# Seven block products for both MLP weights of a hybrid decoder step, with the combinations left in running PSUM banks, on one core

## The chip, the core and the metric

One core of one Trainium2 chip runs the whole program. The metric is the device time of one execution in microseconds (us). Five engines work side by side and wait for one another by semaphores: TensorE (PE, with its weight loads as PEld), VectorE (DVE), ScalarE (ACT), GpSimd (POOL) and SyncE (SP), which issues the transfers. Each of them takes its own instructions strictly in the order in which the program holds them.

## The reference, cut to what matters

One layer over 512 prompt tokens and 64 sample tokens, 576 in all. Two mixers come first and write one matrix; the change touches what follows it.

```python
D_MODEL = 1024
D_FF = 4 * D_MODEL
...
    h1 = x + jnp.concatenate([oa, ob], axis=-1) @ w_o
    hid = jnp.square(jax.nn.relu(rmsnorm(h1, norm2_g) @ w_up))
    y = h1 + hid @ w_down
    return y, kb, vb, s_new, conv_new
```

## The kernel before, in words

Everything is kept transposed: features on the 128 partitions, the 576 tokens along the row, in two halves of 288 (`HALF`). A float32 product is made of three matmuls on numbers split in a high part and the rest: high by high, high by low, low by high. ScalarE writes the high part, VectorE or GpSimd subtracts it to get the low one. A matmul is 128x128 weights by 288 tokens.

**w_up by seven products.** `up(u)` (L1711) makes 256 rows of the hidden layer, for u = 0 to 15. The weights of a unit are seen as 2x2 blocks A11, A12, A21, A22 and the tokens and features as a 2x2 block matrix too, and Winograd's form of Strassen's rule gives the four results from seven products and some sums. The sums of the weights, S1 to S4, are made by GpSimd in `sums_splitter` (L407), four additions of 256 columns for each loaded chunk; `two_parts` (L432) then splits the chunk (1024 columns) and its sums (768) in high and low. The sums of the activations are made once, in `x_factors` (L1619), out of four quadrants `q[0]` to `q[3]` per pair of features i = 0 to 3; `x_parts` (L1641) splits them into the tiles `xf`. Each of the seven products is accumulated over i in a PSUM bank of its own, and `up_out` (L1737) combines them on VectorE, one addition from PSUM per bank. `up_square` (L1757) applies the token scale S and the relu in one VectorE instruction, squares on ScalarE and splits the result into `hid`.

**w_down plainly.** For each 512 hidden rows c and each 128 output rows and half, 12 matmuls run in one bank, and `add_down` (L1776) adds the bank to the residual `h1` on VectorE.

**Order.** The kernel writes its instructions through a class `Flow`, which keeps a clock for each engine by a table of costs and always issues the task that could start first; so the order on each engine is fixed when the program is built. In the MLP the order of the units is two ups, then d(c-2) and two ups in turn, and two downs at the end. Buffers come from pools with caps by use: `mr` for loaded weight chunks, `ms` for weight sums, `q` for quadrants, `g` for PSUM banks (8).

The stage ahead of the MLP is `proj_o`, the product with w_o. Its outputs go through `after_o` (L1560), which adds to `h1`, scales into the quadrants `xq`, and sums the squares for the norm with GpSimd (`acc`, `sq`). So the sums that `up(0)` needs are made while PE still runs `proj_o`.

Of the kernel before, what the change touches and what calls it, by code (L numbers as in the profile page):

```python
# [11 lines left out]
F32R = mybir.dt.float32r  # L12
# [200 lines left out]
def hymba_step(ctx: ExitStack, tc: tile.TileContext, a):  # L213
# [93 lines left out]
    def pool_tt(out, x, y, op, mark=None):  # L307
        fl.op("POOL", 135 + size(x) / 0.47, lambda: nc.gpsimd.tensor_tensor(out, x, y, op=op), mark)  # L308
# [11 lines left out]
    def dma(dst, src, mark=None, slow=1):  # L320
# [17 lines left out]
                      "mr": 2, "ms": 2, "mh": 2, "mg": 2, "ml": 2, "mm": 2})  # L338
# [32 lines left out]
    order = [("u", 0), ("u", 1)]  # L371
    for c in range(2, 8):
        order += [("d", c - 2), ("u", c)]
    order += [("d", 6), ("d", 7)]
    for kind, c in order:
        for i in range(4):
            chunk[kind, c, i] = len(items)
            if kind == "u":
                m, k = 4 * c + i // 2 * 2, i % 2 * 512
                items.append((a["wu"][m:m + 2, :, k:k + 512].rearrange("m p k -> p m k"), 1024))  # L380
            else:
                items.append((a["wd"][c, i], 1024))
    ups = {chunk["u", c, i] for c in range(8) for i in range(4)}
    raw = {}

    def load_w(i):
        src, cols = items[i]
        r = yield from get("wr" if i < MLP else "mr", MID, "wr")
        d = r[:, :cols]
        if len(src.shape) == 3:  # L390
            d = d.rearrange("p (m k) -> p m k", m=src.shape[1])
        dma(d, src, lambda t: raw.update({i: (r, t)}))
# [14 lines left out]
    def sums_splitter():  # L407


        yield lambda: "S" in done  # L410
        for i in range(MLP, len(items)):
            up = i in ups
            if up:
                s = yield from get("ms", MID, "ws")
            yield lambda: i in raw
            r, t = raw.pop(i)
            fl.at(t)
            if up:
                x = r.rearrange("p (m i k c) -> p m k i c", m=2, i=2, k=2)
                A11, A12, A21, A22 = (x[:, j // 2, j % 2] for j in range(4))  # L420
                x = s[:, :768].rearrange("p (j i c) -> p j i c", j=3, i=2)
                S1, S2, S4 = (x[:, j] for j in range(3))
                pool_tt(S1, A21, A22, OP.add)
                pool_tt(A21, A11, A21, OP.subtract)
                pool_tt(S2, S1, A11, OP.subtract)
                pool_tt(S4, A12, S2, OP.subtract)
                fl.spawn(two_parts(i, r, s))
            else:
                fl.spawn(two_parts(i, r, None))
            yield 0  # L430

    def two_parts(i, r, s):  # L432
        out = []
        if i >= MLP + 1 and ("split", i - 1) not in done:
            yield lambda: ("split", i - 1) in done
        for x, n, uh, ul in ((r, 1024, "mh", "ml"), (s, 768, "mg", "mm")):
            if x is not None:
                h = yield from get(uh, MID, "wh", F32R)
                l = yield from get(ul, MID, "wl", F32R)
                act(h[:, :n], x[:, :n])  # L440
                out.append((x, n, h, l))
        sig(("split", i))
        yield 0
        for x, n, h, l in out:
            tt(l[:, :n], x[:, :n], f(h[:, :n]), OP.subtract)
        rel("mr")
        if s is not None:
            rel("ms")
        mark(ready, i, [(h, l) for x, n, h, l in out])

    def splitter():
        for i, (src, cols) in enumerate(items[:MLP]):
# [11 lines left out]
            rel("wr")  # L464

# [1144 lines left out]
    def quad(name):  # L1610
# [3 lines left out]
        return Quad(t)  # L1614


    xf = {}

    def x_factors(i):  # L1619

# [311 lines left out]
```

## Time and profile before

| what | value |
|---|---|
| median of 3 runs (lowest, highest) | 839.0 us (837.73, 839.65) |
| the profiled execution | 836.92 us, span 835.1 us |
| PE busy | 794.9 us, 95% of the span |
| VectorE busy | 569.1 us, 68% |
| ScalarE busy | 342.0 us, 41% |
| GpSimd busy | 276.2 us, 33% |
| granted TensorE clock, mean | 0.982 |

The table is an average over stages. The profiled execution took 1.8 us more than its span, which is what lies around the program, and 2.1 us less than the median. A matmul's busy time covers its way through the array (about 295 ns), so matmuls overlap and PE's rate is read from how many start in a stretch.

### The profile page before, as it was taken

Reading aid. Unit: us, or ns where it says so; the run is one execution under the profiler, and the core shown is the slowest. Engines: PE = TensorE matmul, PEld = TensorE weight load, DVE = VectorE, ACT = ScalarE, POOL = GpSimd, SP = SyncE. Lnnn points to the kernel's source line nnn. Section 1 sums busy time; section 2 is a strip of 40 time slices with the busy share of each in tenths; the row PEclk is TensorE's granted clock in tenths of the full one; section 3 lists DMA queues with packets and bytes.
Section 4 is the critical chain, followed back from the end, with each engine's and each line's share of the span. In section 5 each row is a group of like instructions: output and inputs, shape, how many; then the busy total and the mean of one; then the engine's idle time right before and its main releaser. Section 6 shows DMA issues by size and latency. Waiting matters only on the chain.

```text
span 835.1 us, 15803 instructions
## 1 busy us (share of the span) xinstructions
PE 794.9 (95%) x6299; PEld 730.8 (88%) x6299; DVE 569.1 (68%) x1144; ACT 342.0 (41%) x660; POOL 276.2 (33%) x294
## 2 busy tenths in 40 slices
PE   9999988999999999999866899999999999999998
PEld 8877877878777887879856899999999999999998
DVE  4467278787777875686757785767768586766743
ACT  6538354654232154443552551434325243333410
POOL 4443222243323000132998622233332323333000
PEclk9999999999999999999987999999999999999999
DMA  7722411116778894223002131412223131313312
GB/s 264 150 82 75 151 52 40 46 60 236 254 291 249 292 317 174 108 82 127 26 1 76 53 125 51 139 58 96 88 77 127 51 127 51 126 52 101 127 51 89
DMA packets 53961, 99.05 MB, mean 119 GB/s; under 512 B 12864, under 2 KB 26304, under 8 KB 53888
## 3 DMA queue, kind: packets, MB, share of 16 engines
q1 hardware_dynamic: 53888, 98.05, 35.8%
q8 instruction: 49, 0.80, 0.4%
q14 instruction: 24, 0.20, 0.1%
HBM read 88.15 MB, written 9.69 MB: 117 GB/s over the span
## 4 chain that ended last, share of the span: by engine, by line
PE 72%; POOL 8%; DVE 7%; issue 5%; DMA 4%; ACT 3%; SPq 2%; POOLq 0%; ACTq 0%; DVEq 0%
PE pg L262 52%; PE pa L262 7%; POOL xq L308 3%; SPq L321 2%; POOL acc L308 2%; PE cha L262 2%; DVE y L285 2%; DMA morekv<-in_ck_dram 1%; DMA wr<-in_wk_dram 1%; PE os L262 1%; POOL ws L308 1%; PE ptp L265 1%; PE sc L262 1%; PE cs L262 1%; PE s L262 1%
## 5 line engine op out<-in xcount | busy, mean ns | idle before, releaser
L262 PE MATMUL pg<-hid,wh 128*128 128x288 f32 x1024 | 203.7, 294 | 0.0
L262 PE MATMUL pg<-xf,wh 128*128 128x288 f32 x896 | 183.9, 300 | 8.0 <-DVE xf L278 7.8
L262 PEld LDWEIGHTS pg<-hid,wh 128*128 128x128 f32 x1024 | 164.1, 188 | 0.0
L262 PEld LDWEIGHTS pg<-xf,wh 128*128 128x128 f32 x896 | 147.3, 192 | 9.0 <-DVE xf L278 8.3
L262 PE MATMUL pg<-hid,wl 128*128 128x288 f32 x512 | 151.0, 295 | 0.0
L270 ACT ACTIVATE wh<-wr 128x1024 fp32r<-128x1024 f32 (+1 forms) x104 | 105.1, 1018 | 105.8 <-PE pg L262 46.7
L262 PE MATMUL pg<-xf,wl 128*128 128x288 f32 x448 | 134.5, 300 | 9.5 <-DVE wl L278 9.5
L278 DVE TENSOR_TENSOR h<-pg,h 128x288 f32<-128x288 f32 x160 | 72.5, 454 | 96.7 <-PE pg L262 96.7
L278 DVE TENSOR_TENSOR wl<-wr,wh 128x1024 fp32r<-128x1024 f32 (+1 forms) x89 | 116.6, 1311 | 27.2 <-ACT wh L270 26.7
L308 POOL TENSOR_TENSOR ws<-wr 128x256 f32<-128x256 f32 x32 | 28.8, 900 | 203.5 <-DMA wr<-in_wu_dram 101.2
L262 PEld LDWEIGHTS pg<-hid,wl 128*128 128x128 f32 x512 | 96.1, 188 | 0.0
L262 PEld LDWEIGHTS pg<-xf,wl 128*128 128x128 f32 x448 | 86.1, 192 | 9.9 <-DVE wl L278 9.9
L262 PE MATMUL pg<-xh,wl 128*128 128x288 f32 x256 | 78.1, 305 | 0.0
L262 PE MATMUL pg<-xl,wh 128*128 128x288 f32 x256 | 78.1, 305 | 0.0
L262 PE MATMUL pg<-xh,wh 128*128 128x288 f32 x256 | 78.1, 305 | 0.0
L308 POOL TENSOR_TENSOR wl<-wr,wh 128x1024 fp32r<-128x1024 f32 x15 | 35.9, 2391 | 82.9 <-ACT wh L270 66.3
L278 DVE TENSOR_TENSOR uq<-pg,uq 128x288 f32<-128x288 f32 x96 | 42.2, 454 | 15.6 <-PE pg L262 13.7
L262 PEld LDWEIGHTS pg<-xh,wh 128*128 128x128 f32 x256 | 48.6, 190 | 3.2 <-issue 3.0
L262 PEld LDWEIGHTS pg<-xh,wl 128*128 128x128 f32 x256 | 48.7, 190 | 2.8 <-issue 2.4
L262 PEld LDWEIGHTS pg<-xl,wh 128*128 128x128 f32 x256 | 48.6, 190 | 2.5 <-issue 1.9
L270 ACT ACTIVATE uq<-uq 128x576 f32<-128x576 f32 x32 | 22.0, 686 | 61.7 <-DVE uq L285 61.6
L270 ACT ACTIVATE wh<-ws 128x768 fp32r<-128x768 f32 x32 | 26.9, 840 | 45.6 <-POOL ws L308 17.5
(297 smaller groups left out, 1545.9 us busy)
## 6 DMA issues: line engine op xcount, KB each, us to landing
wr<-in_wu_dram SPq DMA_DIRECT2D x32, 512.0 KB, 3.9
wr<-in_wd_dram SPq DMA_DIRECT2D x32, 512.0 KB, 3.3
morekv<-in_ck_dram SPq DMA_DIRECT2D x20, 512.0 KB, 5.2
morekv<-in_cv_dram SPq DMA_DIRECT2D x20, 512.0 KB, 5.5
wr<-in_wb_dram SPq DMA_DIRECT2D x16, 512.0 KB, 3.8
wr<-in_wo_dram SPq DMA_DIRECT2D x8, 512.0 KB, 5.6
xr<-in_xT_dram SPq DMA_DIRECT2D x8, 288.0 KB, 5.4
h<-in_xT_dram SPq DMA_DIRECT2D x8, 288.0 KB, 6.7
```

The costliest lines, as they stand in the source:

```text
L262: lambda: nc.tensor.matmul(out, lhsT, rhs, start=start, stop=stop, skip_group_check=True))
L265: fl.op("PE", (97, 230), lambda: nc.tensor.transpose(out, in_, ident[:k, :k]))
L270: fl.op("ACT", cost, lambda: nc.scalar.activation(out, in_, func, bias=bias, scale=scale, accum_out=accum), mark)
L278: dve(lambda: nc.vector.tensor_tensor(out, x, y, op=op), out, x, mark=mark)
L285: dve(lambda: nc.vector.scalar_tensor_tensor(out, x, s, y, op0=op0, op1=op1), out, x, 61 if ap(s) else 0, mark=mark)
L308: fl.op("POOL", 135 + size(x) / 0.47, lambda: nc.gpsimd.tensor_tensor(out, x, y, op=op), mark)
L321: fl.op("SP", 4 * slow * size(dst) * dst.shape[0] / 360.0, lambda: nc.sync.dma_start(dst, src), mark)
```

## The change: what it does

Both weights go by seven products now. `down(c, d)` does for 512 hidden rows and 512 output rows what `up` does: two blocks x, seven products each. The products of a pair are no longer seven banks that VectorE combines: product 1 runs in bank A, is read out, product 6 is accumulated on top of it, is read out, then 7, then 4; bank B takes 2, a second bank B takes 5 and then 3 (`seen` makes PE wait for the read). So three banks serve a pair, the order of the products is 1, 2, 6, 5, 7, 3, 4, and each read-out is one result or one term of it.

The weights are split product by product: `part` turns 512 columns into one tile `mw`, high part in front and low part behind, for each of the seven products; `sums` makes S1 to S4 on GpSimd in four additions of 512 columns. The hidden layer needs sums of its quadrants now (`t_sums`), four per unit; `either_tt` puts each on GpSimd or VectorE, by the scheduler's clocks at that moment, as it does the adding of products 1 and 6 of a `down` to `h1`. The first unit (`CLASSICAL = 1`) goes by all eight products, with the loop over i outside, and needs no sums. The scaling of the quadrants by S, eight GpSimd instructions of 576 columns, becomes sixteen VectorE instructions of 288. w_down's chunks come in two transfers of 256 KB each.

```diff
+    def either_tt(out, x, y, op):
+        n = size(x)
+        if fl.free["POOL"] + 1.4 * (135 + n / 0.47) <= max(fl.free["DVE"], fl.now) + 68 + n / 0.96 + 2000:
+            pool_tt(out, x, y, op, slow=1.4)
+        else:
+            tt(out, x, y, op)
...
-                      "mr": 2, "ms": 2, "mh": 2, "mg": 2, "ml": 2, "mm": 2})
+                      "mr": 2, "ms": 2, "mw": 6})
...
+    PO = (1, 2, 6, 5, 7, 3, 4)
+    OF_W = {1: "A11", 2: "A12", 3: "S4", 4: "A22", 5: "S1", 6: "S2", 7: "S3"}
+    CLASSICAL = 1
...
+    def sums(g, A, S):
+        s = yield from get("ms", MID, "ws")
+        t = yield from get("ms", MID, "ws")
...
+        for k, x, y, op in (("S1", "A21", "A22", OP.add), ("S2", "S1", "A11", OP.subtract),
+                            ("S3", "A11", "A21", OP.subtract), ("S4", "A12", "S2", OP.subtract)):
+            X = {**A, **S}
+            pool_tt(S[k], X[x], X[y], op, slow=1.5)
+            mark(sums_at, (g, k), 0)
+            yield 0
+    def part(key, w, x):
+        if key[1] in (3, 5, 6, 7):
+            fl.at(sums_at[key[0], OF_W[key[1]]][1])
+        act(four(w[:, :512]), x)
+        yield 0
+        tt(four(w[:, 512:]), x, four(f(w[:, :512])), OP.subtract)
+        mark(wready, key, w)
...
+    def t_sums(x, key):
+        q = x.q
+        either_tt(q[4], q[2], q[0], OP.subtract)
+        yield 0
+        either_tt(q[5], q[3], q[4], OP.subtract)
+        yield 0
+        fl.spawn(x_parts(x, key, 4, 2), "tsum")
+        either_tt(q[6], q[3], q[2], OP.subtract)
+        yield 0
+        either_tt(q[7], q[1], q[5], OP.subtract)
...
     def x_factors(i):
...
-            pool_tt(x.two(hf), x.two(hf), both(st2["S"], hf), OP.mult)
...
+    def seen(key):
+        if key not in read:
+            yield lambda: key in read
+        fl.at(read[key][1] + LAG)
...
     def up(u):
...
+            if p in (2, 5):
+                B = yield from get("g", [128, 288], "pg")
+            if p in (6, 7, 3, 4):
+                yield from seen(("u", u, {6: 1, 7: 6, 4: 7, 3: 5}[p]))
+            P = B if p in (2, 5, 3) else A
...
     def up_out(u, p, P):
+        if p in (1, 6, 5):
+            act(q[{1: 4, 6: 5, 5: 6}[p]], P)
...
+        o, i, n = {2: (0, 4, 1), 7: (3, 6, 5), 3: (2, 5, 6)}[p]
+        tt(q[o], P, q[i], OP.add)
...
+        stt(q[o], q[o], 0.0, st2["S"][:, c0:c1], OP.max, OP.mult)
...
+    def down_out(g, x, p, P, s):
+        if p in (1, 6):
+            act(s, P)
+            mark(read, key(p), 0)
+            yield 0
+            r, hf = 0, p // 6
+            o = y(r, hf)
+            either_tt(o, o, s, OP.add)
...
+            r, hf = {2: (0, 0), 5: (1, 1), 7: (1, 1), 3: (0, 1), 4: (1, 0)}[p]
+            tt(y(r, hf), P, y(r, hf), OP.add)
```

How the order changes on the engines, as the built programs hold it. First GpSimd, in the middle of the MLP before: `ws` are weight sums, `wr` a loaded chunk.

```order
L308 TENSOR_TENSOR ws<-wr 128x256
L308 TENSOR_TENSOR wr<-wr 128x2x128
L308 TENSOR_TENSOR ws<-ws,wr 128x256
L308 TENSOR_TENSOR ws<-wr,ws 128x256
L308 TENSOR_TENSOR ws<-wr 128x256
```

The four rows come once per chunk of w_up, 32 times, and nothing else of GpSimd's stands between them. The same engine after, between a `down` and an `up`; `uq` are quadrants of a hidden unit, `h` residual rows, `dq` products read out of PSUM.

```order
L308 TENSOR_TENSOR h_3747<-h_3747,dq 128x288
L308 TENSOR_TENSOR h_3787<-h_3787,dq 128x288
L308 TENSOR_TENSOR ws<-ws,wr 128x512
L308 TENSOR_TENSOR ws<-wr 128x512
L308 TENSOR_TENSOR uq<-uq 128x288
L308 TENSOR_TENSOR ws<-wr,ws 128x512
L308 TENSOR_TENSOR uq<-uq 128x288 x2
L308 TENSOR_TENSOR ws<-wr 128x512
L308 TENSOR_TENSOR uq<-uq 128x288
```

Sums of twice the width now stand between additions for the hidden units and the residual: in the whole MLP 124 of 512 columns and 126 of 288, where there were 128 of 256.

VectorE, in the middle of the MLP before, from the end of a `down` to an `up`; `wl` are low parts of weights, `pg` PSUM banks, S the token scale.

```order
L278 TENSOR_TENSOR wl<-wr,wh 128x1024
L278 TENSOR_TENSOR wl<-ws,wh 128x768
L278 TENSOR_TENSOR uq<-pg,uq 128x288 x3
L278 TENSOR_TENSOR uq<-uq,pg 128x288
L285 SCALAR_TENSOR_TENSOR uq<-uq,S 128x576
L278 TENSOR_TENSOR uq<-pg,uq 128x288 x3
L278 TENSOR_TENSOR hid<-uq,hid 128x2x288
```

The same engine after, in an `up`; `mw` is a product's weights, high and low.

```order
L278 TENSOR_TENSOR mw<-ws,mw 128x512 x3
L278 TENSOR_TENSOR hid<-uq,hid 128x576
L278 TENSOR_TENSOR uq<-pg,uq 128x288
L278 TENSOR_TENSOR hid<-uq,hid 128x288
L285 SCALAR_TENSOR_TENSOR uq<-uq,S 128x288
L278 TENSOR_TENSOR mw<-ws,mw 128x512
L278 TENSOR_TENSOR mw<-wr,mw 128x512 x3
L278 TENSOR_TENSOR uq<-pg,uq 128x288
L285 SCALAR_TENSOR_TENSOR uq<-uq,S 128x288
```

Per unit seven additions from PSUM become three and one scaling from PSUM; the low parts, the scalings and the splits of `hid` are more instructions of a smaller width.

PE, at the beginning of `up(0)` before; `xf_4543` and `xf_4544` are the high parts for i = 0, 1 and i = 2, 3 (the low ones are `xf_4545` and `xf_4546`).

```order
L262 MATMUL pg<-xf_4543,wl 128x288
L262 MATMUL pg<-xf_4544,wh 128x288
L262 MATMUL pg<-xf_4546,wh 128x288
L262 MATMUL pg<-xf_4544,wl 128x288
L262 MATMUL pg<-xf_4544,wh 128x288
```

These rows stand after 42 matmuls on i = 0 and 1, where PE turns to i = 2 and 3. The same place after, from the last row of `proj_o` on; each `xf` now holds one i, high and low.

```order
L262 MATMUL pg<-moa,wl 128x288
L262 MATMUL pg<-xf_4539,mw 128x288 x24
L262 MATMUL pg<-xf_4540,mw 128x288 x24
L262 MATMUL pg<-xf_4541,mw 128x288 x24
L262 MATMUL pg<-xf_4542,mw 128x288 x24
L262 MATMUL pg<-xf_4539,mw 128x288 x3
```

The first unit takes its factors in the order in which they are made, one i after the other, and only the second goes through them product by product.

## Rows read from the trace of the kernel before

**Rows 1.** The page's table of engines: busy us (share of span), instructions.
```profile
PE 794.9 (95%) x6299; PEld 730.8 (88%) x6299; DVE 569.1 (68%) x1144; ACT 342.0 (41%) x660; POOL 276.2 (33%) x294
```

**Rows 2.** The chain that ended last, its end: start us, us, what.
```profile
470.47 361.31 PE pg L262 x2710
...
831.80 0.46 DVE h L278
```

**Rows 3.** Busy us (instructions) by stretch, then PE clock, DMA share, GB/s.
```profile
core 0: us, PE busy (x) PEld busy (x) DVE busy (x) ACT busy (x) POOL busy (x), PEclk, DMA share, GB/s
395.00:447.60 52.60, 34.71 (x220) 33.16 (x220) 35.45 (x37) 27.30 (x53) 50.01 (x44) 0.80 0.07 21
447.60:480.00 32.40, 28.68 (x190) 27.86 (x190) 22.10 (x34) 14.64 (x22) 21.51 (x24) 0.90 0.21 66
480.00:820.00 340.00, 340.00 (x2565) 340.00 (x2565) 232.40 (x357) 121.44 (x151) 92.80 (x98) 1.00 0.28 91
```

**Rows 4.** PE in order of time, 428.7 to 446: start, us, [idle before <-releaser].
```profile
436.28 0.61 PE L262 MATMUL pg<-xf,wl 128*128 128x288 f32 x1 [6.33 <-DVE wl L278]
...
445.04 0.61 PE L262 MATMUL pg<-xf,wh 128*128 128x288 f32 x1 [7.35 <-DVE xf L278]
```

**Rows 5.** VectorE in order of time, pieces from 432 to 549.
```profile
432.51 1.98 DVE L278 TENSOR_TENSOR xf<-xq,xf 128x576 fp32r<-128x576 f32 x1 [3.02 <-ACT xf L270]
434.41 1.81 DVE L278 TENSOR_TENSOR wl<-wr,wh 128x1024 fp32r<-128x1024 f32 x1
...
520.17 1.36 DVE L278 TENSOR_TENSOR wl<-wr,wh 128x1024 fp32r<-128x1024 f32 x1
521.46 1.50 DVE L278 TENSOR_TENSOR wl<-ws,wh 128x768 fp32r<-128x768 f32 x1
...
544.28 0.75 DVE L285 SCALAR_TENSOR_TENSOR uq<-uq,S 128x576 f32<-128x576 f32 x1
544.95 1.77 DVE L278 TENSOR_TENSOR wl<-wr,wh 128x1024 fp32r<-128x1024 f32 x1
546.64 0.44 DVE L278 TENSOR_TENSOR h<-pg,h 128x288 f32<-128x288 f32 x1
547.01 0.92 DVE L278 TENSOR_TENSOR hid<-uq,hid 128x576 fp32r<-128x576 f32 x1
```

**Rows 6.** GpSimd in order of time, the same pieces.
```profile
433.83 1.30 POOL L308 TENSOR_TENSOR acc<-acc,sq 128x288 f32<-128x288 f32 x1
435.10 2.39 POOL L308 TENSOR_TENSOR xq<-xq,S 128x576 f32<-128x576 f32 x1
...
520.53 1.60 POOL L308 TENSOR_TENSOR wr<-wr 128x256 f32<-128x256 f32 x1
...
523.63 0.73 POOL L308 TENSOR_TENSOR ws<-wr,ws 128x256 f32<-128x256 f32 x1
...
544.64 0.99 POOL L308 TENSOR_TENSOR ws<-wr 128x256 f32<-128x256 f32 x1 [15.41 <-DMA wr<-in_wu_dram]
545.72 1.60 POOL L308 TENSOR_TENSOR wr<-wr 128x256 f32<-128x256 f32 x1
```

**Rows 7.** VectorE's groups by shape, 480 to 820: busy us, mean ns.
```profile
L278 DVE TENSOR_TENSOR h<-pg,h 128x288 f32<-128x288 f32 x120 | 54.5, 454 | 73.9 <-PE pg L262 73.9
```

**Rows 8.** GpSimd's groups by shape, 395 to 447.6.
```profile
L308 POOL TENSOR_TENSOR xq<-xq 128x288 f32<-128x288 f32 x16 | 17.8, 1129 | 0.3
L308 POOL TENSOR_TENSOR xq<-xq,S 128x576 f32<-128x576 f32 x8 | 13.6, 1696 | 2.0 <-ACT xq L270 2.0
L308 POOL TENSOR_TENSOR acc<-acc,sq 128x288 f32<-128x288 f32 x11 | 12.5, 1140 | 0.0
```

**Rows 9.** VectorE's groups by shape, 395 to 447.6.
```profile
L278 DVE TENSOR_TENSOR xf<-xq,xf 128x576 fp32r<-128x576 f32 x12 | 15.5, 1308 | 7.6 <-ACT xf L270 7.6
L278 DVE TENSOR_TENSOR wl<-wr,wh 128x1024 fp32r<-128x1024 f32 x4 | 6.6, 1642 | 0.0
L278 DVE TENSOR_TENSOR wl<-ws,wh 128x768 fp32r<-128x768 f32 x3 | 5.3, 1757 | 0.0
```

More of the change, by code (lines that the diff above doesn't have):

```diff
@@ L432, in two_parts @@
[L432 to L442, printed above, removed]
-        yield 0
[L444 to L449, printed above, removed]
+    PO = (1, 2, 6, 5, 7, 3, 4)
@@ L1619, in x_factors, with x_parts, have @@
+    def x_parts(x, key, j, n):
+        s, t = x.t[j // 2][:, j % 2 * 288:(j % 2 + n) * 288], x.out
+        act(high(t, j, n), s)
+        yield 0
+        tt(low(t, j, n), s, f(high(t, j, n)), OP.subtract)
+        for k in range(j, j + n):
+            mark(parts, key + (k,), 0)
+        yield 0
+    def have(key, js):
+        return all(key + (j,) in parts for j in js)
     def x_factors(i):
-        if i >= 2:
-            yield lambda: ("xf", i - 2) in done
         x = hx[i] = yield from quad("xq")
+        x.out = xf[i]
@@ L1654, in hymba_step @@
-    parts = {}
+        yield from t_sums(x, ("x", i))
+        yield lambda: have(("x", i), range(8))
+        rel("q", "q", "q", "q")
     ims1 = ct([128, 5], "ims1")
@@ L1704, in stats2, with three @@
         rel("k", "k")
-        cap.update(g=8)
         sig("R2b")
-    hid, Q = {}, {}
+    hid, Q, read, left = {}, {}, {}, {}
+    LAG = 240
+    def seen(key):
+        if key not in read:
+            yield lambda: key in read
+        fl.at(read[key][1] + LAG)
+    def three(p, w, c, x, j, first, last):
+        c = slice(c * 128, c * 128 + 128)
+        l = w[:, 512:]
+        mm(p, w[:, c], high(x, j), first, False, extra=8)
+        mm(p, w[:, c], low(x, j), False, False, extra=8)
+        mm(p, l[:, c], high(x, j), False, last, extra=8)
@@ L1774, in up_square @@
-        rel("q", "q", "q", "q")
-    def add_down(m, hf, p, last):
-        c0, c1 = HALF[hf]
-        tt(h1[m][:, c0:c1], p, h1[m][:, c0:c1], OP.add)
-        rel("g")
-        if last:
-            yield 0
-            dma(a["yT"][:, m, c0:c1], h1[m][:, c0:c1])
+        sig(("Q", u))
+        for hf in (0, 1):
+            yield lambda: all(("relu", u, hf, r) in done for r in range(2))
+            d = x.t[hf][:, :576]
+            act(d, d, AF.Square)
+        yield 0
+        x.out = hid[u] = yield from get("big", [128, 4608], "hid", F32R)
@@ new lines, in up_square, with down @@
+        fl.spawn(x_parts(x, ("h", u), 0, 2))
+        fl.spawn(x_parts(x, ("h", u), 3, 1))
+        yield from t_sums(x, ("h", u))
+        yield lambda: have(("h", u), OF_X.values())
+        rel("q", "q", "q", "q")
+    def down(c, d):
+        A, B = {}, {}
+        g = ("d", c, d)
+        s = yield from get("q", [128, NT], "dq")
+        for p in PO:
+            w = yield from weights(g, p)
+            for x in range(2):
+                if p in (1,):
+                    A[x] = yield from get("g", [128, 288], "pg")
+                if p in (2, 5):
+                    B[x] = yield from get("g", [128, 288], "pg")
+                if p in (6, 7, 3, 4):
+                    yield from seen(g + (x, {6: 1, 7: 6, 4: 7, 3: 5}[p]))
+                P = B[x] if p in (2, 5, 3) else A[x]
+                for i in range(2):
+                    j = OF_X[p]
+                    yield from factor(("h", 2 * c + i), j)
+                    three(P, w, 2 * x + i, hid[2 * c + i], j, i == 0 and p in (1, 2, 5), i == 1)
+                    yield 0
+                fl.spawn(down_out(g, x, p, P, blk(s, x)), "out")
+            rel("mw")
```

322 lines of the change are left out of this document (180 added, 142 removed).

## The prediction

> **What bounds the kernel now.** I read the page first: PE is busy 95% of the span, GpSimd 33% [rows 1]. Then the end of the chain of waits: from 470.47 us one unbroken run of 2710 matmuls, and after the last of them only one addition and the transfer out [rows 2]. So the MLP is bound by PE. The view by stretches gives its rate: 2565 matmuls in 340 us, 132.6 ns each at clock 1.00, while VectorE is busy 232.4 us, ScalarE 121.4 and GpSimd 92.8 [rows 3]. On those numbers fewer matmuls shorten the kernel and the others have room.
>
> Ahead of it lies a stretch that is not PE's. From 395 to 447.6 PE is busy 34.7 of 52.6 us at clock 0.80, GpSimd 50.0 [rows 3]; PE stands for 6.33 and 7.35 us there, for VectorE's low parts [rows 4]. Its cause decides this case. In [rows 5, 6] the reader should lay VectorE's and GpSimd's instructions side by side. An addition of 256 columns on GpSimd takes 0.73 us by itself (523.63) and 1.60 us at 520.53; it ends at 522.13, which is 0.60 after VectorE's low part of 520.17 ended (521.53). VectorE's next one then ends at 522.96, 0.83 after GpSimd's end. At 544.64 GpSimd ends at 545.63, VectorE's low part 1.09 later (546.72), GpSimd's next 0.60 later (547.32), VectorE's next 0.61 later (547.93). So an instruction of VectorE with both operands in SBUF and one of GpSimd never go on together: each finishes a full hold after the other's end. The addition from PSUM at 546.64 takes 0.44 under a running GpSimd instruction, and 120 of its kind 454 ns on the mean [rows 7]: with an operand in PSUM nothing is waited for.
>
> **Holds.** From [rows 5, 6], as the time from the other's end to the own one. GpSimd: 256 columns 0.60; 288 columns 0.64 (435.13 after 434.49); 576 columns 1.27 (437.49 after 436.22); between the last two, an estimate for 512 columns of 1.13. VectorE: 1024 columns 1.09, 768 0.83, 576 0.61; by their slope of 1.07 ns a column, 512 columns 0.54 and 288 columns 0.30. Shapes of 512 don't stand in the trace of before, so these two are the estimates on which the sum turns; the bounds are below.
>
> **The change part by part.**
>
> PE. w_down loses 1536 - 16x84 = 192 matmuls, the first unit gains 12. 180 fewer at 132.6 ns are 23.9 us, if PE stays the bound. An `up` or a `down` of 84 matmuls needs 11.13 us, the two together (a pair) 22.27.
>
> Shared holds of a pair, counted from the code and the order. `up`, GpSimd: four sums of 512 and four of 288 columns, 4x1.13 + 4x0.64 = 7.08. VectorE: seven low parts of 512, three of 576 and one of 288 for `hid`, three scalings of 288, 7x0.54 + 3x0.61 + 4x0.30 = 6.81. `down`: GpSimd 7.08 again (four sums, four additions of products 1 and 6), VectorE 3.78 for seven low parts. 24.75 us a pair, against 22.27 for PE. Before, two ups and one d (the work of two pairs, 360 matmuls, 47.7 us) held 16x0.60 on GpSimd, and on VectorE eight low parts of 1024 (8x1.09), four of 768 (4x0.83) and eight instructions of 576 (8x0.61): 26.5 us, 56% of PE's time. After it is 111%. The shared holds become the bound; that is the forecast.
>
> VectorE's own time. It starts its next instruction 0.67 us after one of 576 columns (544.28 to 544.95) and 0.37 after one from PSUM (546.64 to 547.01) [rows 5], 0.06 above the hold; so 0.60 for 512 and 0.37 for 288. `up`: 7x0.60 + 3x0.67 + 4x0.37, and four reads of PSUM at 0.37: 9.17. `down`: 4.20 and ten reads of PSUM: 7.90. 17.07 a pair. GpSimd's 14.16 us of holds can hide under VectorE's reads of PSUM alone (14x0.37 = 5.2); the rest, 9.0, VectorE waits. 26.0 us a pair, if it never idles for anything else.
>
> The start. From 395 to 447.6 the holds were, by [rows 8, 9]: GpSimd 16x0.64 + 8x1.27 + 11x0.64 and the other 9 of its 44 instructions, of 256 columns, 5.4: 32.8; VectorE 12x0.61 + 4x1.09 + 3x0.83 and three of 288: 15.1. 47.9 of 52.6 us, 91%. So that is how well two saturated engines share. After, the order has ahead of the last quadrants that `up(0)` needs: GpSimd 12 sums and 9 squares of 288 and two sums of 512, 15.7; VectorE 16 scalings of 288, 13 splits of 576, three low parts of 1024 and six of 512, 19.2. 34.9 at 91% is 38.4, to 433.4. Then the last quarter of `up(0)`, 24 matmuls, at the lower clock level (half rate) 6.4: `up(0)` ends near 440, and some 9 us of holds are still owed (four sums, five squares, three splits, 7.6; the first unit's own 4.7; less 3.4 made ahead for the second). Before, 2796 matmuls remained after it, 370.7 us back from the last one: 461. The start gives 21 us.
>
> The sum. 15 ups and 16 downs are 15.5 pairs. From 440: 15.5x26.0 + 9 = 412, to 852; then as before 3.3 us from the last addition (831.80) to the span's end and 1.8 around the span. 857 against the profiled 836.9, 20 us slower. The bounds of that term: holds packed without a gap, 15.5x24.75 + 9 = 393, to 833 and 838 in all; holds at the 91% of the start, 431, to 876 in all. I take 857, between them, because VectorE's reads of PSUM are spread through every unit [rows 7], as cover for GpSimd needs, and were few in the start.
>
> The Trainium skill, "SBUF — State Buffer", section "SBUF: two separate sides", calls the ports that VectorE (with two SBUF inputs) and GpSimd share an exclusive lock: who starts first has it for the whole instruction, the other fully blocks. The trace agrees in kind, but the blocked one ends 0.60 us after the release, not its whole 0.73. If all of an instruction lay behind the release, each of the 16 GpSimd instructions of a pair would hold 0.13 longer, and the packed sum would be 15.5x26.8 + 9 = 424, 869 in all, in place of 838.
>
> The rest costs nothing while its cover lasts. ScalarE's seven high parts and its reads of 288 columns: it is busy 36% of the MLP now [rows 3], and even doubled it stays under a pair; without that cover its extra work would stand on PE's path. Transfers in halves: share 0.28 of the queues [rows 3], loaded a unit ahead; uncovered, one more landing per chunk. The norm's scaling R2 is needed only by the first reads.
>
> **The rivals.**
>
> (a) PE stays the bound: the two engines overlap more than I count. 440 + 15.5x22.27 = 785, 790 in all. For it: PE is never late from 480 on [rows 3], and GpSimd works only 27% there. Against: every pair of rows above. It decides if a pair's holds come to 22.3 or less, that is if a sum of 512 columns holds under 0.82 us in place of 1.13.
>
> (b) The hand-back of a bank. PE may go on in a bank only after the read. Between a product and its successor in the bank lie 12 matmuls in `up` (1.59 us), 18 in `down` (2.39). ScalarE reads seven of the twelve in a pair and doesn't share holds; VectorE reads five, one in `up` and four in `down`. If two blocked low parts (2x1.67) stand ahead of the read (0.45), PE is late by 2.2 and 1.4 us, 7.8 a pair. What is queued behind PE is every later product. Half of that on top of PE's 22.27 is 26.2, no more than the forecast; all of it 30.1, 15.5x30.1 + 9 = 476, 921 in all; three quarters 28.1, 890. It decides above 3.7 us a pair.
>
> (c) PE's clock. In the gaps its granted clock may fall, as in the start: 0.80 with PE busy 66%, 0.90 with 89% [rows 3]. At 0.80 a pair takes 27.8 us, 885 in all. In the forecast PE is busy 86%; it decides below a mean of 0.86.
>
> (d) The scheduler's order packs the holds as if without a gap: 838, no change or a hair faster.
>
> **How the numbers follow.** The forecast, 841 to 880, 62%; (a) 7%, (b) 12%, (c) 10%, (d) 9%, of which I give 5 to faster and 4 to no change. The median of the runs shown is 2.1 above the profiled execution, so I predict 859. 832 to 892 leaves out (a) and the far part of (b) and (c). A run of this kernel can tell 0.2% from no change: faster 0.12, same 0.04, slower 0.84.
>
> **What would show it.** GpSimd busy over 85% of the MLP (14.2 of holds, and waiting for VectorE in between); its 512-column sums near 1.7 us on the mean, VectorE's 512-column low parts near 1.2 in place of 0.68; both nearer their own time would prove (a). PE busy some 86% from 450 on, its gaps ended by VectorE: by `mw` if the low parts are late, by readers of `pg` if (b) is right. Clock near 1.00; under 0.9 speaks for (c). PE at the second unit by 440 to 447. Wrong it would be if the holds of 512 columns are shorter than read off, or if VectorE idles for ScalarE or PE and the holds fit in those gaps.

## The result, and the profile after

The changed kernel takes 898.0 us (median), the one before 839.25 beside it: a ratio of 1.069, with an interval of 1.065 to 1.073. The prediction was 859, so the direction is right and the loss is three times as large, 59 us in place of 20. Of its four executions one, at 915.8, ran at a lower clock (0.932, the others 0.949 to 0.957) and is left out of the ratio. The profiled execution took 899.43, its span is 897.7.

The page's table of engines, and the shares of the chain that ended last, as [rows 1]:

```profile
PE 806.5 (90%) x6119; PEld 731.5 (81%) x6119; DVE 719.0 (80%) x1317; ACT 418.3 (47%) x910; POOL 476.9 (53%) x407
...
PE 43%; DVE 26%; POOL 11%; issue 9%; ACT 7%; DMA 3%; SPq 0%; DVEq 0%; POOLq 0%; ACTq 0%
```

The chain's last 100 us, where [rows 2] had one run of 2710 matmuls:

```profile
789.04 2.94 POOL ws L308 x2
798.87 3.12 DVE mw L278 x4
817.01 4.64 DVE mw L278 x3
822.08 3.26 PE pg L262 x12
...
858.89 35.44 PE pg L262 x264
```

PE bounds only the last stretch, where only `down`s are left (GpSimd still makes sums until 883.8); before it weight sums and low parts stand in the chain. By stretches, with the columns of [rows 3]; the first matmul of the second unit starts at 441.7, the last one ends at 894.3:

```profile
395.00:441.70 46.70, 40.01 (x268) 39.00 (x268) 43.22 (x56) 27.44 (x55) 36.49 (x28) 0.89 0.07 24
480.00:820.00 340.00, 295.59 (x2016) 286.28 (x2016) 305.84 (x419) 162.22 (x322) 253.59 (x190) 0.93 0.23 75
...
441.70:894.30 452.60, 387.31 (x2621) 375.74 (x2619) 402.59 (x553) 213.71 (x424) 332.50 (x253) 0.92 0.23 75
```

In 340 us PE runs 2016 matmuls where it ran 2565. It is busy 87% of them (86% was predicted), VectorE 90%, GpSimd 75% at a granted clock of 0.93. PE's waits from 441.7 to 894.3 (us, times, longest) add up to 64 us:

```profile
PE pg L262 <- DVE uq L278: 28.7, 10, 4.6
PE pg L262 <- ACT uq L270: 18.8, 11, 4.1
PE pg L262 <- ACT dq L270: 8.7, 3, 7.9
PE pg L262 <- DVE mw L278: 4.2, 3, 2.5
PE pg L262 <- DVE h L278: 3.8, 7, 1.6
```

Most of them are waits for somebody who reads a bank (`uq`, `dq`, `h`), which looks like rival (b). The groups by shape, 480 to 820 (busy us, mean ns, idle before), show something else:

```profile
L278 DVE TENSOR_TENSOR mw<-wr,mw 128x512 fp32r<-128x512 f32 x72 | 90.0, 1279 | 0.6 <-ACT mw L270 0.6
L278 DVE TENSOR_TENSOR mw<-ws,mw 128x512 fp32r<-128x512 f32 x95 | 85.8, 912 | 17.1 <-ACT mw L270 16.9
L308 POOL TENSOR_TENSOR ws<-wr 128x512 f32<-128x512 f32 x48 | 77.2, 1608 | 17.0 <-issue 9.5 <-DVE mw L278 6.7 <-PE pg L262 0.7
L308 POOL TENSOR_TENSOR h<-h,dq 128x288 f32<-128x288 f32 x47 | 54.4, 1176 | 48.3 <-ACT dq L270 45.6 <-ACT mw L270 2.6
L278 DVE TENSOR_TENSOR h<-pg,h 128x288 f32<-128x288 f32 x120 | 51.0, 447 | 8.5 <-POOL h L308 3.7 <-PE pg L262 3.4 <-POOL ws L308 0.3
L308 POOL TENSOR_TENSOR uq<-uq 128x288 f32<-128x288 f32 x47 | 50.6, 1081 | 23.6 <-ACT uq L270 22.5 <-DVE uq L278 0.4
```

What has both operands in SBUF takes longer than by itself (a low part of 512 columns that nothing holds up takes 0.69, at 523.02 in the next piece), and the addition from PSUM stays at 447 ns, as in [rows 7]. VectorE in order of time from the end of an `up` on, then GpSimd:

```profile
523.02 0.69 DVE L278 TENSOR_TENSOR mw<-ws,mw 128x512 fp32r<-128x512 f32 x1 [0.94 <-ACT mw L270]
...
529.05 4.64 DVE L278 TENSOR_TENSOR mw<-wr,mw 128x512 fp32r<-128x512 f32 x3
533.62 0.45 DVE L278 TENSOR_TENSOR uq<-pg,uq 128x288 f32<-128x288 f32 x1
534.10 0.46 DVE L285 SCALAR_TENSOR_TENSOR uq<-uq,S 128x288 f32<-128x288 f32 x1
534.48 0.75 DVE L278 TENSOR_TENSOR hid<-uq,hid 128x576 fp32r<-128x576 f32 x1
...
537.41 0.46 DVE L285 SCALAR_TENSOR_TENSOR uq<-pg,S 128x288 f32<-128x288 f32 x1 [1.32 <-PE pg L262]
```

```profile
529.75 1.72 POOL L308 TENSOR_TENSOR ws<-wr 128x512 f32<-128x512 f32 x1
531.44 1.70 POOL L308 TENSOR_TENSOR ws<-wr,ws 128x512 f32<-128x512 f32 x1
541.14 2.02 POOL L308 TENSOR_TENSOR h<-h,dq 128x288 f32<-128x288 f32 x2 [7.99 <-ACT dq L270]
```

Two lessons stand in these rows. GpSimd's two sums end at 531.47 and 533.14, 1.67 apart, with one low part of VectorE's between them: the predicted holds, 1.13 + 0.54, are 1.67. And the low part ends at 533.69, 0.55 after the sum. But then, from 533.14 to 541.14, GpSimd stands 8 us for a product that ScalarE has yet to read out, and VectorE, which now never waits for it, has little that is ready: its instructions that share fill 4.8 of the 8 us. For the rest the shared resource lies idle. Laying all instructions of the two engines over each other from 441.7 to 894.3, I find 409.7 us in which at least one of them is in an instruction that holds or waits for it, 23.5 in which VectorE reads PSUM while GpSimd is idle, and 19.4 in which both are idle. The first figure is nearly the 412 that the prediction gave to this part, with every read of PSUM covered and no idling; the other 43 are the miss. VectorE itself idles 50.0 us there, mostly for these:

```profile
DVE mw L278 <- ACT mw L270: 18.4, 20, 1.5
DVE h L278 <- PE pg L262: 6.9, 21, 1.0
DVE uq L285 <- PE pg L262: 6.3, 6, 1.3
DVE h L278 <- POOL h L308: 5.2, 6, 1.6
DVE uq L285 <- ACT S L270: 3.3, 1, 3.3
DVE hid L278 <- ACT hid L270: 3.1, 5, 0.7
DVE uq L278 <- PE pg L262: 1.8, 1, 1.8
```

### The profile page after: what moved, and what is told of

The parts are those of the page before. It is cut to its first block, busy times and chain, and to the rows that moved or that the text cites. A ratio compares the mean times of both kernels' runs of the same rounds, so it can differ in the third digit from the quotient of the medians.

```text
span 897.7 us, 16132 instructions
## 1 busy us (share of the span) xinstructions
PE 806.5 (90%) x6119; PEld 731.5 (81%) x6119; DVE 719.0 (80%) x1317; ACT 418.3 (47%) x910; POOL 476.9 (53%) x407
## 4 chain that ended last, share of the span: by engine, by line
PE 43%; DVE 26%; POOL 11%; issue 9%; ACT 7%; DMA 3%; SPq 0%; DVEq 0%; POOLq 0%; ACTq 0%
PE pg L262 23%; DVE mw L278 9%; PE pa L262 7%; POOL ws L308 6%; DVE hid L278 3%; DVE y L285 3%; POOL h L308 3%; DVE uq L285 2%; ACT mw L270 1%; PE cha L262 1%; DVE uq L278 1%; DVE h L278 1%; DMA wr<-in_wk_dram 1%; ACT uq L270 1%; POOL uq L308 1%
## 5 line engine op out<-in xcount | busy, mean ns | idle before, releaser
L262 PE MATMUL pg<-xf,mw 128*128 128x288 f32 x1356 | 214.2, 321 | 58.3 <-DVE uq L278 28.7
L262 PEld LDWEIGHTS pg<-xf,mw 128*128 128x128 f32 x1356 | 204.5, 210 | 66.1 <-DVE uq L278 31.8
L262 PE MATMUL pg<-hid,mw 128*128 128x288 f32 x1344 | 190.2, 302 | 13.3 <-ACT dq L270 8.7
L262 PEld LDWEIGHTS pg<-hid,mw 128*128 128x128 f32 x1344 | 185.6, 194 | 17.5 <-ACT dq L270 9.5
L278 DVE TENSOR_TENSOR mw<-ws,mw 128x512 fp32r<-128x512 f32 x124 | 115.1, 938 | 17.6 <-ACT mw L270 17.4
L270 ACT ACTIVATE mw<-ws 128x512 fp32r<-128x512 f32 x124 | 74.7, 624 | 102.6 <-POOL ws L308 79.4
L278 DVE TENSOR_TENSOR mw<-wr,mw 128x512 fp32r<-128x512 f32 x97 | 118.7, 1251 | 1.0 <-ACT mw L270 1.0
L308 POOL TENSOR_TENSOR ws<-wr 128x512 f32<-128x512 f32 x62 | 98.7, 1593 | 30.3 <-DVE mw L278 10.3
L308 POOL TENSOR_TENSOR h<-h,dq 128x288 f32<-128x288 f32 x63 | 71.9, 1160 | 54.0 <-ACT dq L270 48.7
L308 POOL TENSOR_TENSOR uq<-uq 128x288 f32<-128x288 f32 x63 | 68.0, 1086 | 32.4 <-ACT uq L270 31.3
```

The lines of the kernel that those rows point to most:

```text
L262: lambda: nc.tensor.matmul(out, lhsT, rhs, start=start, stop=stop, skip_group_check=True))
L270: fl.op("ACT", cost, lambda: nc.scalar.activation(out, in_, func, bias=bias, scale=scale, accum_out=accum), mark)
L278: dve(lambda: nc.vector.tensor_tensor(out, x, y, op=op), out, x, mark=mark)
L308: fl.op("POOL", (135 + size(x) / 0.47) * slow, lambda: nc.gpsimd.tensor_tensor(out, x, y, op=op), mark)
```

## The experiments

My theory was the one on record: the shared holds (*ports*). Its rivals were the *hand-back* of a running bank (b) and, once that had fallen, a *chain*: that the sums are late for those who wait for them, and their load matters little. All runs are compared by T, from the second unit's first matmul to the last matmul, since in e5 to e9, e12, e13 and e16 the granted clock was 0.61 to 0.80 between 300 and 350 us, ahead of the MLP, where the run of after has 1.00; with it the second unit starts later, by 20 us in e5 whose order is that of after, which is in the total and not in T. So where a range was given for the total, T is held against it as well. Apart from e4 and e8, each experiment is one execution. A pair is an `up` and a `down`; where holds are given, they are those measured in after, 1.15 and 0.667 us for GpSimd's 512 and 288 columns, 0.549, 0.615 and 0.317 for VectorE's 512, 576 and 288: 25.3 us a pair, where 24.75 was estimated.

| run | us | T | holds a pair | VectorE busy in T | GpSimd busy in T | clock in T |
|---|---|---|---|---|---|---|
| before | 839 | 379.0 | | 255.5 | 109.3 | 1.00 |
| after | 898 | 452.6 | 25.3 | 402.6 | 332.5 | 0.92 |
| e1 no sums | 809.5 | 366.6 | 16.1 | 308.7 | 129.2 | 0.98 |
| e2 bank per product | 892.9 | 444.3 | 25.3 | 403.3 | 333.3 | 0.95 |
| e3 PSUM additions | 915.6 | 464.9 | 22.7 | 408.1 | 259.7 | 0.92 |
| e5 memsets | 840.0 | 373.3 | 16.1 | 314.3 | 252.7 | 0.98 |
| e6 sums unused | 918.2 | 456.9 | 25.3 | 399.9 | 331.5 | 0.93 |
| e7 order knows holds | 925.3 | 464.4 | 25.3 | 387.7 | 321.9 | 0.90 |
| e9 four tiles | 924.5 | 453.7 | 25.3 | 403.1 | 331.3 | 0.95 |
| e10 seven tiles | 1009.8 | 562.9 | 25.3 | 400.3 | 311.6 | 0.90 |
| e11 no PSUM additions | 889.2 | 445.5 | 25.3 | 356.2 | 328.3 | 0.93 |
| e12 all 288 on VectorE | 928.0 | 453.5 | 22.5 | 431.6 | 195.2 | 0.94 |
| e13 quarter fewer sums | 872.3 | 415.8 | 23.0 | 379.3 | 285.0 | 0.98 |
| e14 half the sums | 841.4 | 393.0 | 20.7 | 355.4 | 229.8 | 0.98 |
| e15 sums on their own | 903.0 | 459.8 | 25.3 | 411.3 | 337.2 | 0.93 |
| e16 later additions | 950.4 | 490.3 | 25.3 | 411.8 | 321.4 | 0.89 |

**e1: no weight sums.** Products 3, 5, 6 and 7 are split from plain blocks.

```diff
...
-            pool_tt(S[k], X[x], X[y], op, slow=1.5)
...
```

> The changed kernel without the weight sums: GpSimd's 124 additions of 512 columns are left out, and the products that should use S1 to S4 split a plain block in their place, so the results are not the reference's; every split, product, read-out and hand-back of a bank is still there. Theory of the shared ports (VectorE with two SBUF operands and GpSimd wait for each other): the holds of an up and a down together fall from 25.3 us (with the holds of the trace of after: GpSimd 512 columns 1.15, 288 columns 0.67; VectorE 512 columns 0.55, 576 columns 0.615, 288 columns 0.32) to 16.1, under PE's 22.3, and PE becomes the bound: 435 + 15.5 x 22.3 + 5, that is 785 to 805 us. Theory of the hand-back (PE is late because only 12 or 18 matmuls lie between a product and its successor in a bank, whatever the other engines do): PE's waits for read-outs stay near 60 us, 860 us or more.

809.5 us, a little over the 785 to 805 of the ports. PE is the bound again, busy 355.5 of 366.6 us. So w_up and w_down by seven with running banks, without the sums, would have been faster than before. With every hand-back still there, it isn't the cause.

**e2: a fresh bank for each product.** Each product takes a new bank, so PE never waits for a read-out to go on in one.

```diff
-                yield from seen(("u", u, {6: 1, 7: 6, 4: 7, 3: 5}[p]))
-            P = B if p in (2, 5, 3) else A
+            P = yield from get("g", [128, 288], "pg")
...
```

> The changed kernel with a fresh PSUM bank for each product: nothing is accumulated on top of an earlier product and PE never waits for a read-out in order to go on in a bank; all read-outs and additions stay as they are, so the combinations are left out of the results. Theory of the shared ports: the holds are the same, so the time is nearly the same, 870 to 895 us, and PE's waits turn to the low parts of the weights. Theory of the hand-back: the 60 us of waits for read-outs and the low clock behind them go, 800 to 835 us.

892.9 us. PE's waits move and hardly shrink; the longest from 440 on:

```profile
PE pg L262 <- DVE mw L278: 41.5, 30, 4.0
PE pg L262 <- ACT mw L270: 8.0, 5, 5.7
```

The readers of banks were only the first to be late. With them out of the way the low parts are what PE waits for, and a pair takes 28.1 in place of 28.6 us. Rival (b) falls as the cause.

**e3: products 1 and 6 of a `down` added from PSUM by VectorE.** GpSimd loses four additions a pair.

```diff
-            act(s, P)
...
-            either_tt(o, o, s, OP.add)
+            tt(y(r, hf), P, y(r, hf), OP.add)
```

> The changed kernel with products 1 and 6 of a down added to h1 by VectorE straight from PSUM, in place of a ScalarE read-out and a GpSimd addition; same results. Shared ports: 2.7 us of holds less for each up and down (25.3 to 22.7), VectorE has 1.5 us more of its own; at the 89% packing of the changed kernel 25.5 us, 441 + 15.5 x 25.5 + 9 + 5, about 850 us (835 to 865). Hand-back: VectorE reads nine hand-backs in place of five, and it is the engine with the longer queue: no gain, 895 us or more.

915.6 us, slower, with 2.7 us fewer holds a pair. The expectation of the ports (835 to 865) fails; that of the hand-back, 895 or more, holds. VectorE's own work rose by 1.5 us a pair, it now reads nine of the twelve hand-backs, and PE waits 41.5 us for its `uq` and 25.9 for its `hid`; which of the two makes the loss is not shown. A count of holds by itself is no forecast when the work goes to VectorE instead.

**e4: w_down by all eight products, without its sums.** `up` stays as changed.

```diff
-            if g[0] == "u" and g[1] < CLASSICAL:
+            if g[0] == "d" or g[1] < CLASSICAL:
...
```

> The changed kernel with w_down by all eight block products and no sums for it (16 x 96 matmuls in place of 16 x 84, no weight sums for w_down and no sums of hidden quadrants); w_up as changed; same results. Shared ports: holds of an up and a down 12.8 us against 23.9 of PE: PE is the bound, 441 + 15.5 x 23.9 + 5, 805 to 825 us, 2 to 4% faster than the kernel before. Hand-back: the waits in the ups (47 of some 60 us) stay, about 860 us.

845.8 us against 842.6, ratio 1.003 (1.000 to 1.007). Nearly all of the 59 us come with w_down. That no gain is left was not expected: T is 395.6 us for the 2796 matmuls that took 379.0 before. The first two of these units take 32.3 us (442.1 to 474.4) where they took 30.2 before (452.8 to 483.0), so the start accounts for 2 of the 16.6. All that follows takes 363.3 in place of 348.8, and there PE waits 10.2 us, in 7 waits, for VectorE's `uq`, the hand-back.

**e5: memsets in the place of sums.** Each sum of 512 columns becomes four GpSimd memsets of 256 into the same tile: the same order and waits, the sums are constants.

```diff
-            pool_tt(S[k], X[x], X[y], op, slow=1.5)
+            def sets(t=S[k]):
+                for h in (0, 2, 0, 2):
+                    nc.gpsimd.memset(t[:, h:h + 2], 0.5)
+            fl.op("POOL", (135 + 512 / 0.47) * 1.5, sets)
```

> The changed kernel with each of GpSimd's 124 additions of 512 columns replaced by four memsets of 256 columns into the same tile, which read nothing from SBUF; the order on every engine and every wait stay as in the changed kernel, the weight sums are constants, so the results are not the reference's. Shared ports: the low parts of VectorE no longer wait for the sums; holds of an up and a down fall to 16.1 us and PE (22.3) is the bound, 800 to 825 us, and the low parts of 512 columns return to about 0.68 us. If it is the chain of buffers and engines in itself (GpSimd makes a unit's sums late, ScalarE and VectorE split them late, PE waits) and not the waiting of the two engines for each other: the memsets take a similar time, 870 us or more.

```profile
L475 POOL MEMSET ws<- 128x256 f32 x432 | 113.2, 310 | 26.3 <-DVE mw L278 20.1 <-PE pg L262 6.2
L278 DVE TENSOR_TENSOR mw<-ws,mw 128x512 fp32r<-128x512 f32 x109 | 82.1, 762 | 10.0 <-ACT mw L270 9.9
L278 DVE TENSOR_TENSOR mw<-wr,mw 128x512 fp32r<-128x512 f32 x81 | 66.1, 842 | 1.7 <-ACT mw L270 1.7
```

A sum's place takes 4x0.31 = 1.24 us of GpSimd, about what a sum takes alone; yet T is 373.3, 79 less than after, and VectorE's low parts fall from 1279 and 912 to 842 and 762 ns (480 to 800). GpSimd's time is not the matter, only what it does in it: the memset's row has no source, so it reads nothing from SBUF. The total, 840.0, is above the range expected for the ports because the second unit starts 20 us later, after the clock of 0.61 between 300 and 350. The Trainium skill, "SBUF — State Buffer", section "SBUF: two separate sides", says that a VectorE instruction with two SBUF inputs contends only with a GpSimd operation that reads SBUF; the trace agrees.

**e6: sums made and not used.** The load stays, the products are split from plain blocks.

```diff
-                fl.spawn(part((g, p), w, S[k] if k[0] == "S" else A[k]))
+                fl.spawn(part((g, p), w, A[{"S1": "A22", "S2": "A11", "S3": "A21", "S4": "A12"}.get(k, k)]))
```

> The changed kernel with all weight sums made by GpSimd as before, at the same places of its queue, but the four products that should use them split a plain block in their place, so nothing waits for the sums and the results are not the reference's. The load on the shared ports is the same (25.3 us of holds for an up and a down). Shared ports as a pure throughput: 880 to 900 us as the changed kernel. Chain (the holds alone would pack closer to 25.3, but each unit's sums, splits and products wait for one another, and the blocked instructions lengthen each step): cutting the chain at the sums lets the engines pack, 845 to 870 us, not under the 849 that holds without a gap give.

918.2 us in all, over both ranges, with the second unit at 456.2; T 456.9 against 452.6. Nothing is split from a sum, and the time is the same, which speaks against the chain. But ScalarE's high parts still wait 80.8 us for GpSimd's `ws`: a tile that GpSimd wrote or read comes back as a tile for split weights, and its next user waits for GpSimd all the same. So this run didn't take away what it was meant to; e15 does.

**e7: a scheduler that knows the waiting.** `Flow` delays an instruction that shares until the other engine's ends.

```diff
+        if c.queue[0][2].__name__ == "port":
+            ahead = self.port
...
+        if emit.__name__ == "port":
+            self.port = t - 60
```

> The changed kernel with another order: the scheduler's clocks now let an instruction of VectorE with both operands in SBUF and one of GpSimd wait for each other, in place of factors 1.4 and 1.5 on GpSimd alone; same instructions but for the choice between GpSimd and VectorE, same results. Shared ports as a pure throughput: 885 to 905 us. Chain: an order made with the real delays puts the reads of PSUM in front of blocked low parts and wins some of the 3 us a pair that are not held by anyone, 855 to 885 us.

925.3 us, T 464.4. The order it writes is worse by 12 us, and no expectation held.

**e8: the parts that gain.** w_down plainly as in e4, a bank per product and VectorE's combinations in `up` as before; new against the kernel before are mainly the split by product, and the first unit by all eight.

```diff
...
+            tt(q[5], P, q[4], OP.add)
...
+            tt(q[7], P, q[5], OP.add)
...
```

> w_down by all eight products as in the run with the plain down, and w_up's seven products each in a bank of its own, combined on VectorE as in the kernel before; first unit by all eight, weights split by product; same results. Expected of all theories of the ports: the holds stay under PE's time, and the 1.0 us that each up lost to the hand-back of banks goes: 442 + 15 x 11.13 + 16 x 12.73 + 5 = 818, with some 5 us lost in the second and third unit 820 to 830 us, 1.5 to 2.5% faster than the kernel before. If the loss in the second and third unit (10 us with the plain down) is of the ports of the start: 830.

831.1 us against 840.2: ratio 0.988 (0.986 to 0.990), 1.2% under the kernel before, and well under the changed one. Against e4, T falls from 395.6 to 379.4. 4 of the 16 us are in the first two units (28.1 for 32.3); the other 12 (351.3 for 363.3) are the price of running banks, so (b) was real where the holds don't cover it. T is as before (379.0, for the same 2796 matmuls), so the gain must lie ahead of the second unit. The trace kept doesn't show it: this execution took 838.3 us, with the clock at 0.80 between 300 and 350 and the second unit at 453.7, against 452.8 before. In e4, with the same first unit and the clock at 1.00 there, the second unit begins at 442.1.

**e9 and e10: four and seven tiles for split weights.** A pair might take longer because PE, ScalarE and VectorE hand six tiles round.

```diff
-                      "mr": 2, "ms": 2, "mw": 6})
+                      "mr": 2, "ms": 2, "mw": 4})
...
```

> The changed kernel with four tiles for split weights in place of six; every instruction and every result stays. Theory of the ports: the shared holds (25.3 us a pair) and VectorE's reads of PSUM set 28.6 us a pair, so two tiles fewer change little: 895 to 905 us. Theory of the ring: a pair takes 28.6 in place of 26.0 because PE, ScalarE and VectorE hand six tiles round, and a late low part comes back as a late high part for VectorE; then four tiles must cost clearly: over 920.

> The changed kernel with seven tiles for split weights, at the price of three in place of four for loaded chunks; all results stay. Theory of the ring: VectorE's 51 us of idle time shrink by a third or more, 875 to 888 us. Theory of the ports: 893 to 905.

With four, T is 453.7, 1 us more than after: there is no such ring. The total of 924.5 would fit it (over 920), but the second unit starts at 465.7 here, 24 us later than in after, behind a clock of 0.64 between 300 and 350. Seven tiles cost a loaded chunk: T 562.9, and PE waits 83.7 us for VectorE's and 46.0 for ScalarE's `mw`. A chunk is held until product 4, a unit's last, so with three the next unit's splitting begins late. That says nothing on the ring.

**e11: w_down's additions from PSUM left out.**

```diff
-            tt(y(r, hf), P, y(r, hf), OP.add)
             mark(read, key(p), 0)
```

> The changed kernel without VectorE's ten additions from PSUM in each down (products 2, 5, 7, 3, 4 are run and not added: left out). The shared holds stay all; VectorE loses 10x0.37 = 3.7 us a pair of work that needs no port, and GpSimd as much cover. Theory of the ports: what VectorE saves it waits instead, 890 to 905 us. Theory of VectorE's queue (what it does in order, ports or not, is the limit): 28.6 falls by 2.5 to 3.7 a pair, 840 to 860 us.

889.2 us, T 445.5. VectorE is busy 46 us less and the time falls by 7. Its own queue isn't the limit in after; most of what it saved it stands idle (89 us for 50), and the low parts wait a little longer (1328 and 988 ns).

**e12: all additions of 288 columns on VectorE.**

```diff
-        if fl.free["POOL"] + 1.4 * (135 + n / 0.47) <= max(fl.free["DVE"], fl.now) + 68 + n / 0.96 + 2000:
-            pool_tt(out, x, y, op, slow=1.4)
-        else:
-            tt(out, x, y, op)
+        tt(out, x, y, op)
```

> The changed kernel with all additions of 288 columns on VectorE, so that GpSimd has only the sums of 512; all results stay. Eight a pair move: the holds fall from 25.3 to 25.3 - 8x0.667 + 8x0.317 = 22.5 us a pair, VectorE's own work rises by 8x0.37 = 3.0. Theory of the ports, at the 88% of now: 25.4 a pair, 845 to 855 us. Theory of VectorE's queue: 28.6 rises by 1 to 3 a pair, 910 to 945.

928.0 us, T 453.5: neither the gain of the one nor the loss of the other. The total lies in the range of VectorE's queue only because the second unit starts at 469.3, behind a clock of 0.68 between 300 and 350. VectorE is busy 431.6 of T, 95%. So the likely reading is that the holds gave way and VectorE took their place; that the time came out the same is chance.

**e13 and e14: fewer sums.** Of a unit's four sums S3, then S3 and S4 are left out (the cut is of e14).

```diff
...
-            pool_tt(S[k], X[x], X[y], op, slow=1.5)
+            if k not in ('S3', 'S4'):
+                pool_tt(S[k], X[x], X[y], op, slow=1.5)
```

> The changed kernel with one of the four weight sums per unit (S3) left out, 31 of 124; its product is split from a plain block, so results differ. Theory of the ports with 88.5% packing: 25.3 - 2x1.15 = 23.0 us of holds a pair, 23.0/0.885 = 26.0, 15.5x26.0 + 9 = 412 in place of 452.6 from the second unit to the last matmul, 855 to 870 us in all. Theory that something else holds a pair at 28.6 (the runs so far lie at 445 to 465 whatever was moved): 445 to 460 for that part, 890 to 910 us.

> As the run before, with two of the four weight sums per unit (S3 and S4) left out, 62 of 124. Ports at 88.5%: 25.3 - 4x1.15 = 20.7 a pair, 23.4, 15.5x23.4 + 9 = 372, 815 to 830 us, near PE's 22.3 a pair. Something else: 445 to 460 for the part from the second unit on, 890 to 910 us.

The part from the second unit on, after, e13 and e14 (columns as [rows 3]):

```profile
441.70:894.30 452.60, 387.31 (x2621) 375.74 (x2619) 402.59 (x553) 213.71 (x424) 332.50 (x253) 0.92 0.23 75
451.40:867.20 415.80, 367.71 (x2621) 355.82 (x2619) 379.31 (x551) 212.64 (x424) 285.02 (x224) 0.98 0.25 81
443.20:836.20 393.00, 364.24 (x2621) 354.56 (x2619) 355.37 (x551) 212.60 (x422) 229.82 (x192) 0.98 0.27 85
```

452.6, 415.8, 393.0, and 366.6 without any (e1). The first 31 sums give back 36.8 us, 1.19 each, for a hold of 1.15: where the holds bound, a sum costs its hold and little more. The next 31 give 22.8, as PE (15.5x22.27 = 345 without a gap) comes near. T of e13 was forecast at 412; e14 came out 21 above the 372 forecast, with two bounds of nearly the same size, 20.7 and 22.3 us a pair. So "something else" falls. But with a sum a wait for it went too, which is why the next run was made.

**e15: the same load, and nobody waits for it.** GpSimd makes its 124 sums from a tile of their own into the same tile; the products are split as in e6.

```diff
-            pool_tt(S[k], X[x], X[y], op, slow=1.5)
+            pool_tt(o, o, q, OP.add, slow=1.5)
...
```

> The changed kernel in which GpSimd's 124 sums of 512 columns are made, in their places in its queue, from a tile of their own into the same tile; nothing waits for them, and no tile that they use comes back as a tile for weights. Products 3, 5, 6 and 7 are split from plain blocks, so results differ. In the run with sums unused ScalarE's high parts still waited 80.8 us for GpSimd, through tiles that came back; here none does. Theory of the ports (the load alone): 440 to 460 us from the second unit to the last matmul, 890 to 925 in all. Theory of the chain (the time is the wait for sums): under 400, and under 855 in all.

903.0 us, T 459.8, and of ScalarE's waits from 438 on these are all that hold up a high part, and `ws` is in none:

```profile
ACT mw L270 <- DVE mw L278: 34.4, 17, 3.6
...
ACT mw L270 <- PE pg L262: 9.7, 9, 2.0
```

The load alone makes the time. e1 splits the same plain blocks and differs in nothing but GpSimd's sums and the order that `Flow` writes without them: 366.6, so 124 sums that nobody uses cost 93 us. With e5, the chain without the load (T 373.3), this is the clearest comparison: it is the holds that bound the changed kernel.

**e16: the additions of products 1 and 6 planned 5 us later**, so that sums go ahead of them in GpSimd's queue.

```diff
+            fl.at(read[key(p)][1] + 5000)
             either_tt(o, o, s, OP.add)
```

> The changed kernel with each addition of a product 1 or 6 to the residual put 5 us later in the scheduler's plan, so that weight sums stand ahead of it in GpSimd's queue; all results stay. In after GpSimd stands 48.7 us for these products in 10 waits. If that stand is what leaves the ports idle: at least 15 us less from the second unit to the last matmul, 437 or under. If another wait takes its place: 445 to 460.

950.4 us, T 490.3, outside both ranges. GpSimd's wait for ScalarE's `dq` is gone, and it stands 64.5 us for VectorE's `h` and 71.7 for PE, before it can write its sums (loaded chunks, sums and split weights take their buffers from one pool); PE waits 50.6 us for ScalarE's `dq`. Another wait took the place, a dearer one.

## Why the prediction was wrong, step by step

**What held.** The mechanism: e5 and e15 show it, and e1, e13 and e14 its size. The holds of 512 columns, 1.15 and 0.549 for the estimates of 1.13 and 0.54, and 25.3 us a pair for 24.75. By the rule of the Trainium skill, "SBUF — State Buffer", section "SBUF: two separate sides", as the prediction put it, GpSimd's sum would have held its whole length, 1.29 where nothing holds it up; the measured 1.15 decides for the sum made from rows. The start: the second unit began at 441.7, for 440. PE's share, 86%; the means, 1608 ns for "near 1.7 us", 912 and 1279 for "near 1.2".

**The step that failed** is the term "26.0 us a pair, if it never idles for anything else". It stood for VectorE's own time and its waits, 15.5x26.0 + 9 = 412. VectorE was indeed busy for 402.6, own time and waits together; but it idles another 50.0 us of the 452.6, and 28.6 us a pair is what came of it. 50.0 less the 9.4 by which it was busy less than 412 is 40.6, the miss (the total is 39 above 859). Of the 50.0 VectorE stood 24.8 for ScalarE, 15.0 for PE and 5.2 for GpSimd, which the prediction itself named as a sign of being wrong; it had put ScalarE's part at nothing, by its busy time alone. The prediction had the right row for this and chose against it: in the start the holds filled 91% [rows 8, 9], and the sum by that was 876. Over the MLP they fill (15.5x25.3 + 9)/452.6 = 89%; in e2, e6, e9, e11 and e15, with other waits, tiles and VectorE work, 87 to 90%, in e13 88%. The reason given for taking the better value, that reads of PSUM cover GpSimd's holds, failed twice: 23.5 us of those reads go by while GpSimd is idle, where none were to, and e11, without most of them, is no slower.

**Rival (b)** explained PE's waits in the trace and not the time: e2 takes it away and 8 us go. Where the holds don't bound, in e4 against e8, it costs 12, and in e3 its expectation held. **Rival (c)**: the clock did fall, to 0.93 from 480 to 820, and PE was busy 387.3 us for 2604 matmuls that at the rate of [rows 3] take 345. It rises to 0.98 as the holds go (e13, e14), so it follows the gaps; whether it also lengthens them was not tried apart. T doesn't follow the clock from run to run: 453.7 at 0.95 in e9, 452.6 at 0.92 in after. **Rivals (a) and (d)** fell with the holds, and with the 11% of the time that they leave empty. GpSimd "over 85%" was wrong for the same reason as the failed step: 75%, since it stands 48.7 us in its queue for products that ScalarE has yet to read out and 31.3 for quadrants (`uq`) of hidden units that ScalarE has yet to finish.

**Still open** is which wait leaves the shared resource idle for 11%. GpSimd's stand of 8 us above is one such place; taking its additions away (e12) brought VectorE to its limit, and moving them back in the queue (e16) made other engines stand instead. Five changes of order, banks and tiles (e2, e7, e9, e11, e16) found no order that fills more than 90%.

## What to carry to other kernels

Where two engines never run together on a kind of instruction, add up their holds per unit of work as if they were one engine, and take the share that such a stretch of the same trace really fills (here 91%), not a packing that a good order might give; above PE's time per unit they are the bound, however idle each looks. Here that count foretold what leaving work out gives (e1, e13), and failed where the work went from one of the two engines to the other (e3, e12). When PE waits for the readers of its banks, take that wait away once: if another takes its place, the first was not the cause. A product saved is worth what its sums leave of it: here the seven products of w_down saved PE 192 matmuls, 25 us, and the kernel lost 52 (e4 against after). What those of w_up are worth, no run tried.

## What the runs showed of the hardware

A blocked instruction ends sooner after the other's release than it takes alone, by 0.13 to 0.14 us on either engine (after, 441.7 to 894.3: VectorE's 512 columns 0.549 for 0.681, GpSimd's 1.150 for 1.289). In e5 GpSimd's memsets of 256 columns took 310 ns on the mean beside VectorE's low parts, which fell toward their own 0.69 us (762 and 842 ns): an operation of GpSimd that doesn't read SBUF hardly held them up; additions of 288 columns stood in between all the while. In e5 to e9, e12, e13 and e16 the granted clock was 0.61 to 0.80 in one stretch of 50 us (300 to 350) with PE busy 46 to 49 of it, and 1.00 there in after and the other runs; what sets it off was not found.
